# A transformer layer on one Trainium2 core: host order of x, norm weight spread by TensorE, and a written order of the engines for the first token tiles

## The chip, the core and the metric

The kernel runs on one core of a Trainium2 chip. The metric is the device time of one execution in microseconds (us); lower is better. The core has TensorE (in the profile PE for matmuls, PEld for the load of their stationary operand), VectorE (DVE), ScalarE (ACT), GpSimd (POOL) and SyncE (SP), which here only issues transfers. Each takes its instructions in order; semaphores join them. A difference of about 0.2% is what measurements of this kernel can tell from none.

## What is computed

One layer of an encoder on 1024 tokens of width 1024, in float32. Cut to what matters here:

```
h = x + 0.5 * swiglu(rms_norm(h, ffn1_norm), w_gate, w_up, w_down)   # d_ff 2816
u = rms_norm(h, mix_norm); two attention branches, gated; h = h + merged @ w_out
h = h + 0.5 * swiglu(rms_norm(h, ffn2_norm), ...)
y = rms_norm(h, final_norm)

swiglu: (silu(x @ w_gate) * (x @ w_up)) @ w_down
rms_norm: x * rsqrt(mean(x*x) + 1e-6) * g
```

The change touches the first norm, the start of the first `x @ w_gate` and `x @ w_up`, and the addresses of x and of the output.

## The kernel before

**Tokens.** The 1024 tokens form a grid of 16 rows and 64 columns. A token tile t (128 tokens) is the block of 8 columns over all rows; its rows of x lie in 16 runs of 8 tokens (L41). The output is written by the same pattern (L42, L1179). `res(t)` (L153) is the home of tile t in SBUF: four tiles `fx`, four quarters of `fa`.

**Precision.** Every operand of a product is kept as two parts: `split` (L88) has ScalarE cast the high part (L89) and VectorE subtract it for the low part (L90). `mm3` (L138) multiplies high by high, high by low, and low by high: three matmuls of 128 x 128 by 128 x 512 (L141, L143, L145) for each 128 of the contraction.

**Products.** The projections go by a Strassen scheme with seven products P1 to P7 (`products`, L233). The right operands are made from the turned, normed tiles: B11 and B21 (tiles 0 to 3) are there first, the others need tiles 4 to 7. For each group i of hidden units and m (gate, up) one product is four times `mm3`. P1 and P2 of groups 0 to 2 come first in the sequence (L239), since they need only B11 and B21. `prep` (L270) loads weights and splits them; for groups 1 and 2 of these the weights come through `ahead` (L261); `run` (L332) preps a little ahead and multiplies.

**The opening.** L590 to L602: SyncE issues x0, the norm weight (read 128 times over, 512 KB, L109), x1 to x3, the first gate and up blocks (`raw`), x4 to x7, and the second gate and up blocks. `transition` (L160) then takes the tiles in turn. `normed` (L112): ScalarE sums squares (L119), GpSimd makes the scale (L122, L123), VectorE multiplies by scale and weight (L125). `to_strassen` (L189): TensorE turns the tile by eight transposes into two banks (`turned`, L129), ScalarE and VectorE split the two banks into B11 and B21, and for tiles 0 to 3 ScalarE also keeps unsplit copies in `res` (L204, L205). For tiles 4 to 7 VectorE forms T1, T2 and what later becomes T3 and T4 (L209 to L215) and each is split. `behind` (L341) lets ten steps of the products run after each tile from tile 3 on. A scheduler puts all this in an order for each engine; engines keep to that order on the chip. `strassen_rest` (L221) and the rest of the products follow.

**Banks.** There are four PSUM banks "d" and four "g"; the turns use "d", the first products "g".

Of the kernel before, what the change touches and what calls it, by code (L numbers as in the profile page):

```python
# [25 lines left out]
NEG = -1.0e30  # L26
BIG = 1.0e38
# [9 lines left out]
def trunk_kernel(ctx, tc, x, n1, wg1, wu1, wd1, nm, win, rpb, sink, wa, wb, wo,  # L37
# [3 lines left out]
    x2 = x.rearrange("o (r b w) d -> (o b) r w d", b=NTT, w=8)  # L41
    out2 = out.rearrange("o (r b w) d -> (o b) r w d", b=NTT, w=8)  # L42
# [69 lines left out]
    def normed(h, gb, xs=None, parts=1):  # L112

        xs = xs4() if xs is None else xs
        w = D // parts
        cols = [slice(i * w, (i + 1) * w) for i in range(parts)]
        st = const.tile([P, 4], F32, tag="st", bufs=4, name=nm_("st"))
        for i, c in enumerate(cols):
            nc.scalar.activation(xs[:, c], h[:, c], AF.Square, scale=D ** -0.5, accum_out=st[:, i:i + 1])  # L119
# [3 lines left out]
        nc.gpsimd.tensor_tensor(st[:, 2:3], st[:, 0:1], nhalf, op=ALU.pow)  # L123
        for c in cols:
            nc.vector.scalar_tensor_tensor(out=xs[:, c], in0=h[:, c], scalar=st[:, 2:3], in1=gb[:, c],  # L125
                                           op0=ALU.mult, op1=ALU.mult)
        return xs

# [31 lines left out]
    def transition(pre, gain, turn_tile, post, halves=1, spare=()):  # L160


        h, xs = {}, {}
        n = NTT // halves
        for base in range(0, NTT, n):
            for t in (base, base + 1):
                h[t] = pre(t)
            xs[base] = normed(h.pop(base), gain)
            yield
            for t in range(base, base + n):  # L170
                if t + 2 < base + n:
                    h[t + 2] = pre(t + 2)
                if t + 1 < base + n:
                    xs[t + 1] = normed(h.pop(t + 1), gain, spare_xs() if t + 1 in spare else None)
# [13 lines left out]

    def to_strassen(t, xs):  # L189
# [5 lines left out]
        def put(o, src, eng=None):  # L195
            h, l = rhs(o)
            split(h[:, :, cols], l[:, :, cols], src, eng)
# [35 lines left out]
    def products(src, n, after, at_end, extra, ring):  # L233
# [36 lines left out]
        def prep(q):  # L270
# [11 lines left out]
            r1, r2 = raws[i, m, 0], raws[i, m, 1]  # L282
            a11, a12, a21, a22 = r1[:, :512], r1[:, 512:], r2[:, :512], r2[:, 512:]
# [13 lines left out]
        def multiply(q):  # L297
            i, p, m = seq[q]
            w = lhs.pop(q)
            h, l = rhs(RIGHT[p])  # L300
            first = p in ("P1", "P2", "P5")
            if p in ("P1", "P6", "P7", "P4"):
                if i == 2 and p == "P6":
                    first = True
                if first:
                    bks[i]["W", m] = bank("d" if i == 2 and p == "P1" else "g")
                b = bks[i]["W", m]
            elif p == "P2":
                if i == 2:
                    bks[i]["X", m] = bks[i]["W", m]  # L310
                    first = False
                else:
# [19 lines left out]
        def run():  # L332
            for q in range(len(seq)):
                prep_until(q + (1 if q < 4 else 2 if q < len(early) else 8))
                yield from multiply(q)
# [3 lines left out]
        return load, prep_until, run(), load_ahead  # L339

    def behind(prods):  # L341

        run, load_ahead = prods[2:]
# [222 lines left out]
    def down_ffn(wd, src):  # L566
# [4 lines left out]
        for t in range(NTT):  # L571
            loads.setdefault(2 + t, []).append(lambda d, t=t: nc.sync.dma_start(res(t), src(t)))
# [11 lines left out]
    down = down_ffn(wd1[0], lambda t: x2[t])  # L584
    hg = hidden(wg1[0], wu1[0], down.at_end)

    def load_x(t):
        nc.sync.dma_start(res(t), x2[t])

    load_x(0)  # L590
    gain = load_gain(n1[0])
    for t in range(1, 4):
        load_x(t)
    for m in range(2):
        hg[0](0, m, 0)
    for t in range(4, NTT):
        load_x(t)
    for m in range(2):
        hg[0](0, m, 1)
    drain(transition(res, gain, to_strassen, behind(hg), spare=(2, 3)))  # L600
# [560 lines left out]
    down = down_ffn(wd2[0], lambda t: h_d[t * P:(t + 1) * P, :])  # L1161
# [13 lines left out]
    def finish(t):  # L1175
        y = normed(res(t), gain, raw4() if t in (5, 7) else None, 2)
        for n in range(2):
            sl = slice(n * 512, (n + 1) * 512)
            nc.sync.dma_start(out2[t][:, :, sl], y[:, sl])  # L1179
# [9 lines left out]
def _consts():  # L1189
# [22 lines left out]
    tok = np.arange(T).reshape(ROWS, NTT, 8)  # L1212
    rope = rope[:, :, tok.transpose(1, 0, 2).reshape(-1)]
# [29 lines left out]
```

## Time and profile before

| | us |
|---|---|
| median of 3 runs | 1969.58 (1968.11 to 1970.52) |
| the profiled execution | 1971.38 |
| its span (first to last instruction) | 1969.4 |
| TensorE busy in the span | 1929.7 |
| VectorE, ScalarE busy | 1435.6, 952.4 |
| first transpose; first product | 9.35; 24.36 |
| last store of the output issued | 1964.78 |

In a row of a timeline the first number is the start in us from the span's start, the second the duration, then engine, line, operation, tile written and tiles read, shape, and in brackets how long the engine had been idle and what ended it. A row with x4 stands for four that follow each other. A group's row (from the page) gives busy time, mean ns, and idle time ahead of it with the releaser. A row of a window gives its stretch, its length, the busy time (and count) of TensorE, its weight load, VectorE, ScalarE and GpSimd, then granted clock, DMA share and GB/s. A row with three durations separated by slashes gives minimum, median and maximum in ns and the first and last start.

### The profile page before, as it was taken

The page shows a single profiled execution, that of the slowest core. Times are in us where ns is not written, and L with a number is a line of the kernel's source. Part 1 is how long each engine was busy: PE and PEld are TensorE (multiplying, and loading weights), DVE is VectorE, ACT ScalarE, POOL GpSimd, SP SyncE. Part 2 cuts the span into 40 slices and gives each one's busy share as a digit, 9 for nine tenths or more (in the row PEclk, how much of TensorE's full clock was granted, in tenths as well). Part 3 has the DMA queues.
Part 4 walks back from the last instruction along what each step waited for, and adds up shares of the span by engine and source line. Part 5 has one row for each costly group of instructions (what it writes and reads, how often), then busy time and mean ns, then how long its engine had stood idle before and what let it go on. Part 6 is the DMA issues. An engine that isn't in the chain of part 4 may idle for free. (4 is left out here: it accounts for less than half of the span.)

```text
span 1969.4 us, 25670 instructions
## 1 busy us (share of the span) xinstructions
PE 1929.7 (98%) x8968; PEld 1608.5 (82%) x8968; DVE 1435.6 (73%) x2503; ACT 952.4 (48%) x1846; POOL 338.1 (17%) x469
## 2 busy tenths in 40 slices
PE   6999999999999999899999999999999999999997
PEld 5888888888888888788888888878888888888886
DVE  6976566558967688578888866989766556569864
ACT  7433333334446543467787873356333333344452
POOL 1010001003400112111022134510101001005110
PEclk9999999999999999999999999999999999999999
DMA  8433323368333568553368675545523332493341
GB/s 210 141 116 102 118 86 107 123 221 271 92 118 124 168 190 268 173 171 94 84 161 176 177 240 192 182 139 156 149 87 107 107 102 95 139 356 105 117 141 53
DMA packets 234784, 293.45 MB, mean 149 GB/s; under 512 B 14208, under 2 KB 161024, under 8 KB 234656
## 3 DMA queue, kind: packets, MB, share of 16 engines
q1 hardware_dynamic: 206816, 206.24, 34.9%
q0 software_dynamic: 27840, 85.58, 13.2%
q8 instruction: 71, 1.16, 0.2%
q14 instruction: 57, 0.47, 0.1%
HBM read 205.16 MB, written 86.70 MB: 148 GB/s over the span
## 5 line engine op out<-in xcount | busy, mean ns | idle before, releaser
L141 PE MATMUL g<-ar,ws 128*128 128x512 f32 x1184 | 444.8, 397 | 3.6 <-ACT xs L870 1.9
L143 PE MATMUL g<-ar,ws 128*128 128x512 f32 x1184 | 438.2, 391 | 0.1
L145 PE MATMUL g<-ar,ws 128*128 128x512 f32 x1184 | 436.5, 391 | 0.3 <-DVE ws L90 0.3
L90 DVE TENSOR_TENSOR ws<-raw,ws 128x512 fp32r<-128x512 f32 (+1 forms) x329 | 237.3, 727 | 177.0 <-ACT ws L89 175.7
L89 ACT CAST ws<-raw 128x512 fp32r<-128x512 f32 (+1 forms) x331 | 209.5, 638 | 295.3 <-PE d L145 122.0
L141 PE MATMUL d<-ar,ws 128*128 128x512 f32 x680 | 262.4, 390 | 0.5 <-ACT ws L89 0.5
L145 PEld LDWEIGHTS g<-ar,ws 128*128 128x128 f32 x1184 | 223.2, 189 | 48.2 <-DVE ws L90 0.7
L145 PE MATMUL d<-ar,ws 128*128 128x512 f32 x680 | 261.9, 389 | 0.6 <-DVE ws L90 0.5
L143 PEld LDWEIGHTS g<-ar,ws 128*128 128x128 f32 x1184 | 223.4, 189 | 47.5 <-DVE ar L90 0.5
L143 PE MATMUL d<-ar,ws 128*128 128x512 f32 x680 | 262.0, 389 | 0.0
L141 PEld LDWEIGHTS g<-ar,ws 128*128 128x128 f32 x1184 | 218.2, 189 | 43.3 <-ACT xs L870 2.7
L145 PEld LDWEIGHTS d<-ar,ws 128*128 128x128 f32 x680 | 127.6, 188 | 27.5 <-DVE ws L90 1.1
L141 PEld LDWEIGHTS d<-ar,ws 128*128 128x128 f32 x680 | 127.6, 188 | 27.5 <-ACT ws L89 1.1
L143 PEld LDWEIGHTS d<-ar,ws 128*128 128x128 f32 x680 | 127.6, 188 | 26.4
L356 POOL DMA_DIRECT2D hid<-fx x96 | 52.1, 542 | 503.6 <-DVE fx L398 379.6
L90 DVE TENSOR_TENSOR ws<-ar,ws 128x512 fp32r<-128x512 f32 x114 | 108.1, 955 | 4.5 <-ACT ws L89 4.5
L89 ACT CAST ar<-raw 128x512 fp32r<-128x512 f32 (+1 forms) x83 | 56.0, 678 | 91.2 <-PE g L143 53.1
L90 DVE TENSOR_TENSOR ws<-fa,ws 128x512 fp32r<-128x512 f32 x76 | 52.6, 692 | 53.3 <-ACT ws L89 52.9
L141 PE MATMUL g<-ws,ws 128*128 128x512 f32 x232 | 91.0, 392 | 0.0
L145 PE MATMUL g<-ws,ws 128*128 128x512 f32 x232 | 90.4, 390 | 0.0
L143 PE MATMUL g<-ws,ws 128*128 128x512 f32 x232 | 90.3, 389 | 0.0
L1016 ACT ACTIVATE fa<-fa,nmx 128x385 f32<-128x385 f32 (+3 forms) x128 | 75.5, 591 | 27.5 <-DVE nmx L1013 26.8
(232 smaller groups left out, 3515.1 us busy)
## 6 DMA issues: line engine op xcount, KB each, us to landing
raw<-hid SPq DMA_DIRECT2D x70, 512.0 KB
hid<-fx POOLq DMA_DIRECT2D x96, 256.0 KB, 2.6
raw<-in_ffn_w_up_dram SPq DMA_DIRECT2D x32, 512.0 KB
ar<-in_ffn_w_down_dram SPq DMA_DIRECT2D x32, 512.0 KB
raw<-in_ffn_w_gate_dram SPq DMA_DIRECT2D x28, 512.0 KB
hid<-fa POOLq DMA_DIRECT2D x54, 256.0 KB, 2.6
raw<-in_w_in_dram SPq DMA_DIRECT2D x27, 512.0 KB
ar<-zs_d POOLq DMA_DIRECT2D x48, 256.0 KB, 5.1
```

The costliest lines, as they stand in the source:

```text
L89: nc.scalar.copy(dst_hi, src)
L90: (eng or nc.vector).tensor_tensor(dst_lo, src, f32v(dst_hi), op=ALU.subtract)
L141: nc.tensor.matmul(b, lhs[0], r[0], start=first, stop=False, **kw)
L143: nc.tensor.matmul(b, lhs[0], r[1], start=False, stop=False, **kw)
L145: nc.tensor.matmul(b, lhs[1], r[0], start=False, stop=last, **kw)
L356: nc.gpsimd.dma_start(hid[PRODUCTS.index(p), i], src)
L1016: nc.scalar.activation(pr, pr, AF.Exp, scale=-1.0, bias=nmx[:, s:s + 1], accum_out=ssum[:, s:s + 1])
```

## The change

1. The host brings x into tile order, so that a tile of x is 128 rows that follow each other, and the host undoes that order on the output. Loads of x (also those for the residual) and stores of the output become plain row ranges.
2. The norm weight of the first norm is loaded as 8 x 128 (4 KB) as the first transfer. TensorE turns it into columns; eight transposes of a column that is read 128 times give the weight for all partitions, and VectorE copies it out of PSUM in two halves. Twelve transposes of the identity stand before and twelve after.
3. x0, x1, the first gate block, x2, x3, the first up block, then x4 to x7 is the order of the first transfers. P1 and P2 of group 0 need no second half of the weights any more; it is loaded after tile 4.
4. The first four products (P1, P2 of group 0, gate and up) are done in two halves of 256 columns: `half(q)` multiplies tiles 0 and 1 only; `run` later does the columns of tiles 2 and 3.
5. For tiles 0 to 3 the order of VectorE, ScalarE and TensorE is written by hand and kept (`first_tiles`); from tile 4 on the scheduler decides.

```diff
+ORDER = np.arange(T).reshape(ROWS, T // P, 8).transpose(1, 0, 2).reshape(-1)
-    x2 = x.rearrange("o (r b w) d -> (o b) r w d", b=NTT, w=8)
-    out2 = out.rearrange("o (r b w) d -> (o b) r w d", b=NTT, w=8)
+    x2 = x.rearrange("b t d -> (b t) d")
+    out2 = out.rearrange("b t d -> (b t) d")
...
-            for half in range(2):
+            for half in range(1 if i == 0 and p in ("P1", "P2") else 2):
                 if (i, m, half) not in raws:
                     load(i, m, half)
...
+            ts = slice(0, 512) if n is None else slice(n * 256, n * 256 + 256)
             for c in range(4):
                 cs = slice(c * P, (c + 1) * P)
-                mm3([b], c == 0 and first, c == 3, (w[:, cs], w[:, 512:][:, cs]),
-                    [(h[:, c, :], l[:, c, :])], skip_group_check=True)
+                mm3([b[:, ts]], c == 0 and first and n != 1, c == 3, (w[:, cs], w[:, 512:][:, cs]),
+                    [(h[:, c, ts], l[:, c, ts])], skip_group_check=True)
...
+            if t == 4:
+                for m in range(2):
+                    prods[0](0, m, 1)
...
+    def first_gain(g):
+        rows = main.tile([NC8, P], F32, tag="s1", bufs=1, name=nm_("rows"))
+        nc.sync.dma_start(rows, g.rearrange("(c f) -> c f", c=NC8))
+        b = bank("g")
+        for _ in range(12):
+            nc.tensor.transpose(b[:, :P], ident, ident)
+        b = bank("d")
+        nc.tensor.transpose(b[:, :NC8], rows, ident[:NC8, :NC8])
+        cols = const.tile([P, NC8], F32, name="cols")
+        nc.vector.tensor_copy(cols, b[:, :NC8])
+        gb = const.tile([P, 1152], F32, tag="gain", bufs=1, name=nm_("gain"))
+        for half in range(2):
+            b = bank("g")
+            for c in range(4):
+                k = 4 * half + c
+                nc.tensor.transpose(b[:, c * P:(c + 1) * P], cols[:, k:k + 1].to_broadcast([P, P]), ident)
+            nc.vector.tensor_copy(gb[:, half * 512:half * 512 + 512], b)
+        b = bank("g")
+        for _ in range(12):
+            nc.tensor.transpose(b[:, :P], ident, ident)
+        return gb[:, :D]
...
+    def first_tiles():
+        st, pts = {}, {}
+        def put(t, o):
+            put_cols((B11, B21)[o], slice(t * P, (t + 1) * P), pts[t][o])
+        def keep(t):
+            for o in range(2):
+                nc.scalar.copy(res(t)[:, o * 512:(o + 1) * 512].rearrange("p (c t) -> p c t", c=4), pts[t][o])
+        def turn(t):
+            pts[t] = turned(scaled(*st[t], res(t), gain))
+        def half(q):
+            hg[1](q + 1)
+            drain(hg[4](q, 0))
+        for t in range(3):
+            st[t] = root(res(t), None if t < 2 else spare_xs())
+        turn(0)
+        put(0, 0)
+        st[3] = root(res(3), spare_xs())
+        turn(1)
+        put(1, 0)
+        for q in range(2):
+            half(q)
+        for t in range(2):
+            put(t, 1)
+            keep(t)
+        turn(2)
+        half(2)
+        put(2, 0)
+        put(2, 1)
+        half(3)
+        turn(3)
+        put(3, 0)
+        put(3, 1)
+        for t in (2, 3):
+            keep(t)
+
+    with tc.manual_schedule(engines={DVE, Activation, PE}):
+        first_tiles()
+    tc.no_sync_barrier()
+    post = behind(hg)
+    xs = {4: normed(res(4), gain)}
+    for t in range(4, NTT):
+        if t + 1 < NTT:
+            xs[t + 1] = normed(res(t + 1), gain)
+        to_strassen(t, xs.pop(t))
+        post(t - 1)
+    post(NTT - 1)
```

Here `root` is the first half of `normed` (ScalarE's sum of squares and GpSimd's scale), `scaled` the second (VectorE's multiplication), and `put_cols` one split of a turned bank into B11 or B21.

More of the change, by code (lines that the diff above doesn't have):

```diff
@@ L123, in normed, with scaled @@
         nc.gpsimd.tensor_tensor(st[:, 2:3], st[:, 0:1], nhalf, op=ALU.pow)
-        for c in cols:
+        return xs, st
+    def scaled(xs, st, h, gb, parts=1):
+        w = D // parts
+        for i in range(parts):
+            c = slice(i * w, (i + 1) * w)
             nc.vector.scalar_tensor_tensor(out=xs[:, c], in0=h[:, c], scalar=st[:, 2:3], in1=gb[:, c],
@@ L304, in multiply @@
                     first = True
-                if first:
+                if first and n != 1:
                     bks[i]["W", m] = bank("d" if i == 2 and p == "P1" else "g")
@@ L583, in trunk_kernel @@
         new_ar(g)
-    down = down_ffn(wd1[0], lambda t: x2[t])
+    down = down_ffn(wd1[0], x2)
     hg = hidden(wg1[0], wu1[0], down.at_end)
     def load_x(t):
[L588 to L592, printed above, removed]
+        nc.sync.dma_start(res(t), x2[t * P:(t + 1) * P, :])
+    def first_gain(g):
[19 more added lines that the diff above has]
+        return gb[:, :D]
@@ L593, in trunk_kernel @@
+    gain = first_gain(n1[0])
+    for t in range(2):
         load_x(t)
-    for m in range(2):
-        hg[0](0, m, 0)
+    hg[0](0, 0, 0)
+    for t in range(2, 4):
+        load_x(t)
+    hg[0](0, 1, 0)
     for t in range(4, NTT):
         load_x(t)
-    for m in range(2):
-        hg[0](0, m, 1)
-    drain(transition(res, gain, to_strassen, behind(hg), spare=(2, 3)))
+    def first_tiles():
[19 more added lines that the diff above has]
+            half(q)
+        for t in range(2):
+            put(t, 1)
[10 more added lines that the diff above has]
+            keep(t)
```

54 lines of the change are left out of this document (32 added, 22 removed).

## The prediction

> **What bounds the kernel now.** I read the page first (how full TensorE is), then TensorE's waits, then the first 51 us engine by engine, because the change touches only these and the last transfers.
>
> ```profile
> span 1969.4 us, 25670 instructions
> PE 1929.7 (98%) x8968; PEld 1608.5 (82%) x8968; DVE 1435.6 (73%) x2503; ACT 952.4 (48%) x1846; POOL 338.1 (17%) x469
> ...
> L145 PE MATMUL d<-ar,ws 128*128 128x512 f32 x680 | 261.9, 389 | 0.6 <-DVE ws L90 0.5
> ```
>
> TensorE is busy for 98% of the span, so the kernel ends earlier or later by what TensorE waits. The L145 row names one wait on VectorE for a weight's low part (DVE ws L90). Its place follows from the timelines of TensorE, VectorE (DVE) and ScalarE (ACT).
>
> ```profile
> 9.35 1.97 PE L134 MATMUL d<-ident,xs 128*128 128x128 f32 x8 [9.35 <-DVE xs L125]
> 18.91 3.83 PE L134 MATMUL d<-ident,xs 128*128 128x128 f32 x16 [3.68 <-ACT fx L204]
> 24.36 0.79 PE L141 MATMUL g<-ar,ws 128*128 128x512 f32 x1 [1.63 <-ACT ar L89]
> 26.88 0.78 PE L143 MATMUL g<-ar,ws 128*128 128x512 f32 x1
> 28.87 0.39 PE L141 MATMUL g<-ar,ws 128*128 128x512 f32 x1
> 29.10 0.40 PE L143 MATMUL g<-ar,ws 128*128 128x512 f32 x1
> 34.34 1.03 PE L134 MATMUL d<-ident,xs 128*128 128x128 f32 x8
> 48.99 1.03 PE L134 MATMUL d<-ident,xs 128*128 128x128 f32 x8
> 50.12 0.50 PE L145 MATMUL d<-ar,ws 128*128 128x512 f32 x1
> ```
>
> ```profile
> 8.01 1.28 DVE L125 SCALAR_TENSOR_TENSOR xs<-fx,st,gain 128x1024 f32<-128x1024 f32 x1 [8.01 <-POOL st L123]
> 17.55 2.48 DVE L90 TENSOR_TENSOR ar<-d,ar 128x512 fp32r<-128x512 f32 x4
> 42.80 1.28 DVE L125 SCALAR_TENSOR_TENSOR xs<-fa,st,gain 128x1024 f32<-128x1024 f32 x1
> 44.00 0.69 DVE L209 TENSOR_TENSOR fa<-d,fx 128x512 f32<-128x512 f32 x1
> 49.38 0.69 DVE L90 TENSOR_TENSOR ws<-ahead,ws 128x512 fp32r<-128x512 f32 x1
> 58.39 0.68 DVE L287 TENSOR_TENSOR s<-raw 128x512 f32<-128x512 f32 x1
> ```
>
> The first product starts at 24.36, the stream holds from 26.88, and matmuls then follow each other every 0.23 us (28.87 to 29.10). At 50.12 it stops once more: the matmul there needs the low part that VectorE makes from 49.38 to 50.07. This is the eighth weight, product P2 of group 1, m = 1. From there to 790 us the waits of TensorE are one row:
>
> ```profile
> PE d L141 <- ACT ws L89: 0.5, 1, 0.5
> ```
>
> So the opening is worth what **VectorE** needs to reach that one subtraction; the start of the first product decides nothing by itself. VectorE's account: in the built order 48 instructions stand from the first norm (8.01) to that subtraction, 8 norms with 1.2 us from one to the next (42.80 to 44.00) and 40 of 512 columns at 0.60 (four in 2.48, the last 0.08 being pipeline): 8 x 1.2 + 40 x 0.6 = 33.6 us. From 8.01 to 50.07 are 42.06, so VectorE idles 8.4 there.
>
> **The change part by part.** The built order of the changed program has the same 48 instructions between the first norm and the low part of the eighth weight (only their order differs; the three new copies of the norm weight stand ahead). After the 147th TensorE instruction of before, at 50.1, TensorE's order is the same to the end. So the sum is: where VectorE starts, 33.6 us of work, and its idle time in the new order.
>
> *Loads.* These rows give ScalarE's waits for x, and the pace of the transfers:
>
> ```profile
> 5.87 1.06 ACT L119 ACTIVATE xs<-fx 128x1024 f32<-128x1024 f32 x1 [3.86 <-DMA fx<-in_x_dram]
> 9.77 1.06 ACT L119 ACTIVATE xs<-fx 128x1024 f32<-128x1024 f32 x1 [2.75 <-DMA fx<-in_x_dram]
> 12.02 1.06 ACT L119 ACTIVATE xs<-fx 128x1024 f32<-128x1024 f32 x1 [1.10 <-DMA fx<-in_x_dram]
> 15.26 1.05 ACT L89 CAST ar<-d 128x512 fp32r<-128x512 f32 x2
> ```
>
> ```profile
> 18.00:24.00 6.00, 3.83 (x16) 3.14 (x16) 4.66 (x9) 5.73 (x12) 0.79 (x2) 1.00 1.04 236
> 26.00:35.00 9.00, 9.00 (x42) 7.63 (x41) 7.65 (x12) 8.02 (x15) 2.35 (x4) 1.00 1.17 287
> 1121.50:1124.50 3.00, 3.00 (x20) 2.69 (x19) 2.77 (x10) 2.39 (x8) 0.57 (x1) 1.00 0.79 298
> 1299.60:1302.00 2.40, 2.40 (x12) 1.97 (x12) 2.40 (x5) 2.40 (x7) 0.80 (x2) 1.00 1.00 403
> ```
>
> ```profile
> 1121.05 0.80 SPq L1103 DMA_DIRECT2D fx<-h_d  x2
> ...
> 1298.80 2.89 SPq L1167 DMA_DIRECT2D h_d<-fx  x4
> ```
>
> A scattered tile of x (512 KB) takes 2.2 us (236 GB/s), a half block of weights 1.8 (287). For a contiguous tile the bounds are 2.2 and 1.3 (the contiguous h_d stores at 403); I take 1.75, from the window that reads h_d back (298). The 512 KB norm weight leaves the head of the queue for a 4 KB one, and the first gate block moves ahead of x2. Landings, from 5.87 for x0 with a little off for its shorter issue: x0 5.6, x1 7.4, gate 9.2, x2 10.95, x3 12.7, up 14.5. The second gate and up halves move behind x and the first blocks ahead; their first reader is P5 (L287 at 58.39), and the e_d copies behind them are read near 960 us, so this costs nothing.
>
> *Norm weight by TensorE.* Nine transposes, a tiny copy and two 512-column copies follow a 4 KB load that lands near 3.7. At 0.22 a transpose (1.97 for eight) and 0.68 a copy they end near 7.7, when the first norm is ready anyway (5.6 + 2.14, the step from 5.87 to 8.01). Nothing on the path: the first tile waits later for another reason, with over 3 us of cover.
>
> *Fixed order.* Here is the cost. Every engine takes its queue in order, and I follow VectorE:
> - norm 0 from 7.8 to 9.0. The next VectorE instruction is the low part of tile 0. It needs ScalarE's high part, which now stands behind the square sum of x2: that starts when x2 lands, 10.95, ends at 12.05, the high part takes 0.6. **Idle 3.65**, to 12.65.
> - norm 1 stands behind it: 13.25 to 14.5. TensorE turns tile 1 (first half after 1.1), ScalarE casts to 16.3: **idle 1.85**. The first product starts at 16.8, 7.6 us before 24.36.
> - Four low parts to 18.7. The fifth needs a cast that stands behind two keep copies, one of which waits for VectorE's own 18.1 to 18.8: **idle 1.2**, to 19.9.
> - norm 2 from 20.5 to 21.8. TensorE turns tile 2 after the 24 half matmuls that stand ahead (16.8 to about 22); turn and cast end at 23.5: **idle 1.15**.
> - norm 3 to 26.6, turn, cast: **idle 1.4**, to 27.9; two low parts to 29.1.
> - norm 4 needs tile 4's square sum, which ScalarE has behind two casts and all four keep copies of tiles 2 and 3 (27.3 to 30.1; two casts take 1.05 at 15.26, so 0.48 from one to the next), though x4 landed near 16. Square sum and GpSimd's steps take 2.14: **idle 3.2**, to 32.3.
> - Then VectorE runs full, but for **1.0** near 44, where ScalarE loads the table for Silu ahead of a cast that VectorE needs (row below), and 0.15 of rests.
>
> ```profile
> L395 ACT ACT_TABLE_LOAD  x2: 1283/1283/1283, 38.1 to 1340.4; - x2
> ```
>
> Idle together 13.6, against 8.4. VectorE reaches the end of that low part at 7.8 + 33.6 + 13.6 = 55.0 instead of 50.07: **+4.9**. TensorE, early with its halves, waits meanwhile: turn 4 (norm 4 ends at 33.6) stands in its queue ahead of 21 half matmuls that are ready, and turn 6 waits for a norm that VectorE does after 2 norms and 8 subtractions (40.8).
>
> *Halves.* 96 matmuls of 256 columns for 48 of 512. Four of 256 columns in the row below give 0.12 each (the row at 1010.87 follows 0.49 later):
>
> ```profile
> 1010.38 0.65 PE L1048 MATMUL g<-ws,fx 128*128 128x256 f32 x4
> 1010.87 0.34 PE L1008 MATMUL d<-ar 128*128 128x384 f32 x1
> ```
>
> 96 x 0.12 - 48 x 0.23 = 0.5 us more work, hidden in TensorE's waits; without these it costs 0.5.
>
> *Warming transposes.* In before 16 transposes run at 0.22 to 0.24 each at 18.91 and the first products come late after each other, too; at 34.34 a transpose takes 0.13. [...] At 0.21 a half matmul turn 2 comes at 22.1 to 22.4, at 0.12 it comes at 21.85, when norm 2 ends: a term of 0.3 to 0.8, not 5.
>
> *Output.* The last two stores decide the end:
>
> ```profile
> 1964.78 1.20 SPq L1179 DMA_DIRECT2D out_dram<-raw  x2
> ```
>
> ```profile
> L663 SPq DMA_DIRECT2D h_d<-fa x4: 319/338/339, 654.0 to 673.3; - x4
> ```
>
> 0.6 us an issue, with a row pattern of three dimensions; contiguous rows take 0.32 to 0.34 in the h_d stores (L663). The last issue can end 0.2 to 0.3 earlier and its packets follow more closely; bounds 0 and 0.9, I take **-0.5**. The second load of x, for the residual, is contiguous now and hidden: between 51 and 790 us TensorE waits for no transfer (the one row above).
>
> Sum +4.9 - 0.5 = +4.4. The profiled execution took 1971.38 (span 1969.4 and 1.98 around it), 1.8 above the median of the runs; the difference is put on the median: 1969.58 + 4.4 = **1974.0**.
>
> **Rivals.**
> *The early start pays* (faster). TensorE alone would need from 16.8 to the place it has at 50.12 the 147 instructions of before less 16 turns done: 83 matmuls x 0.23, 48 transposes x 0.13, some 2.5 for those at the lower clock and 0.5 for the halves = 28.4, so 45.2: -4.9, with the stores -5.4: 1964.2. It decides when VectorE idles under 3.8 us (45.2 - 7.8 - 33.6). For it: the first product does come 7.6 us earlier, and the page calls TensorE the full engine. Against it: the two stalls before norm 4 and behind x2 alone are 6.9. Chance 0.06.
> *Smaller loss*: x at the pace of the stores (three tiles x 0.45: x2 1.35 earlier) and halves at 0.12 (0.3): idle 12.0, so +3.3, +2.8 with the stores: 1972.4. Chance 0.22.
> *Larger loss*: contiguous rows bring nothing (2.2 a tile: x2 1.35 later) and the lower clock lasts past turn 3 (8 transposes and a half product, 0.9): idle 15.8, so +7.1, +6.6 with the stores: 1976.2. Chance 0.14.
> *It does not what it says*: the new order of x moves the same bytes, and the output's order is undone outside; a scheduler that puts the queues otherwise is excluded by the built order. No chance of its own.
>
> **How the numbers follow.** The forecast has 0.58, by itself 1972.9 to 1975.3. The bound of 0.2%, which is what a measurement tells from no change, is 3.9 us: 1973.5. Of the forecast's chance I put 0.44 above it; with the larger loss slower has 0.58, within has 0.36 (0.14 and the smaller loss), faster 0.06. The range is 1971.8 to 1976.8: it leaves out the early start, and the outer part of the two losses.
>
> **What would show it.** Right: the first half matmul near 17; VectorE idle 3 us or more before the norm of tile 4, released by GpSimd behind ScalarE; TensorE waiting before turns 4 and 6, until about 33.6 and 40.8; the last wait of the opening at about 55 on a DVE ws row. Wrong: the low part of the eighth weight before 51 us, or no TensorE wait after 30 us (the early start), or a first norm of tile 1 well before 13 us. If TensorE gains in the opening and the end is still later, a wait beyond 60 us has grown, which the unchanged order there speaks against.

## The result, and the profile after

The changed kernel takes 1975.29 us (median of 7 runs, 1973.82 to 1979.87), the kernel before 1969.58 beside it: a ratio of 1.0033, 95% interval 1.0021 to 1.0045. It is slower, by 5.7 us between the medians. The profiled execution took 1975.28 with a span of 1973.1, against 1971.38 and 1969.4: +3.9.

The page of the changed kernel, as of before:

```profile
span 1973.1 us, 25840 instructions
PE 1936.7 (98%) x9049; PEld 1614.8 (82%) x9049; DVE 1437.2 (73%) x2506; ACT 952.3 (48%) x1846; POOL 340.3 (17%) x469
```

TensorE still fills 98% of the span. Its waits between 62 and 790 us are again next to nothing (waits of TensorE in that stretch):

```profile
PE g L152 <- DVE fa L752: 0.2, 1, 0.2
```

So the opening is where to look, and there VectorE. These are the rows of its timeline that begin with an idle stretch, and the last one is the low part of the eighth weight (49.38 in before):

```profile
7.32 1.28 DVE L132 SCALAR_TENSOR_TENSOR xs<-fx,st,gain 128x1024 f32<-128x1024 f32 x1 [0.21 <-POOL st L125]
11.30 0.69 DVE L92 TENSOR_TENSOR ar<-d,ar 128x512 fp32r<-128x512 f32 x1 [2.69 <-ACT ar L91]
...
15.00 0.69 DVE L92 TENSOR_TENSOR ar<-d,ar 128x512 fp32r<-128x512 f32 x1 [1.82 <-ACT ar L91]
...
18.64 0.69 DVE L92 TENSOR_TENSOR ar<-d,ar 128x512 fp32r<-128x512 f32 x1 [1.14 <-ACT ar L91]
...
21.96 1.29 DVE L92 TENSOR_TENSOR ar<-d,ar 128x512 fp32r<-128x512 f32 x2 [0.76 <-ACT ar L91]
...
26.47 1.29 DVE L92 TENSOR_TENSOR ar<-d,ar 128x512 fp32r<-128x512 f32 x2 [1.43 <-ACT ar L91]
30.92 1.28 DVE L132 SCALAR_TENSOR_TENSOR xs<-fa,st,gain 128x1024 f32<-128x1024 f32 x1 [3.16 <-POOL st L125]
32.97 1.28 DVE L132 SCALAR_TENSOR_TENSOR xs<-fa,st,gain 128x1024 f32<-128x1024 f32 x1 [0.77 <-POOL st L125]
...
44.29 0.69 DVE L92 TENSOR_TENSOR ar<-fa,ar 128x512 fp32r<-128x512 f32 x1 [1.04 <-ACT ar L91]
...
51.22 0.69 DVE L92 TENSOR_TENSOR ar<-fa,ar 128x512 fp32r<-128x512 f32 x1 [0.23 <-ACT ar L91]
...
54.23 0.68 DVE L92 TENSOR_TENSOR ws<-ahead,ws 128x512 fp32r<-128x512 f32 x1
```

It starts 54.23 - 49.38 = 4.85 later than before. The idle stretches behind norm 0 add up to 13.0, and nearly all end on ScalarE or on a scale that waits for ScalarE. ScalarE's timeline has two of the causes:

```profile
9.64 1.06 ACT L121 ACTIVATE xs<-fx 128x1024 f32<-128x1024 f32 x1 [2.15 <-DMA fx<-in_x_dram]
...
10.70 0.57 ACT L91 CAST ar<-d 128x512 fp32r<-128x512 f32 x1
...
26.81 2.07 ACT L654 COPY fx<-d 128x512 f32<-128x512 f32 x4
28.72 1.11 ACT L121 ACTIVATE xs<-fa 128x1024 f32<-128x1024 f32 x1
```

The high part of tile 0 (10.70) stands behind the square sum of x2, which waits for its transfer until 9.64 (1.3 of the 2.69; the rest, 1.37 in e2 below, is the turn and the cast). The square sum of tile 4 (28.72) stands behind the four keep copies.

TensorE's timeline shows the clock by the pace of equal instructions:

```profile
6.22 1.47 PE L632 MATMUL g<-ident 128*128 128x128 f32 x12
8.66 1.09 PE L145 MATMUL d<-ident,xs 128*128 128x128 f32 x8 [0.97 <-DVE xs L132]
13.23 1.97 PE L145 MATMUL d<-ident,xs 128*128 128x128 f32 x8 [3.48 <-DVE xs L132]
15.54 0.58 PE L152 MATMUL g<-ar,ws 128*128 128x256 f32 x1 [0.34 <-ACT ws L91]
...
18.87 0.41 PE L154 MATMUL g<-ar,ws 128*128 128x256 f32 x1
19.08 0.41 PE L156 MATMUL g<-ar,ws 128*128 128x256 f32 x1
...
22.05 0.28 PE L154 MATMUL g<-ar,ws 128*128 128x256 f32 x1
22.17 0.28 PE L156 MATMUL g<-ar,ws 128*128 128x256 f32 x1
...
32.35 1.06 PE L145 MATMUL d<-ident,xs 128*128 128x128 f32 x8 [1.75 <-DVE xs L132]
...
40.40 1.94 PE L145 MATMUL d<-ident,xs 128*128 128x128 f32 x8 [2.79 <-DVE xs L132]
...
54.97 0.50 PE L156 MATMUL d<-ar,ws 128*128 128x512 f32 x1 [0.48 <-DVE ws L92]
```

Twelve transposes at 6.22 take 1.47 (0.12 each) and turn 0 takes 1.09: full pace. TensorE then idles 3.48, and turn 1 takes 1.97 again; half matmuls follow each other every 0.21 until about 19.6 and every 0.12 from then on. The last three rows are TensorE's waits for VectorE ahead of turn 4, of turn 6 and of the product with the eighth weight. Windows of the same kernel, whose third number from the end is the granted clock:

```profile
12.90:19.60 6.70, 6.01 (x25) 5.32 (x26) 3.73 (x7) 4.40 (x9) 0.93 (x2) 0.50 1.08 356
...
39.00:40.00 1.00, 0.00 (x0) 0.00 (x0) 1.00 (x2) 1.00 (x3) 0.92 (x2) 1.00 0.00 0
40.20:43.40 3.20, 3.00 (x11) 2.76 (x12) 3.05 (x6) 3.17 (x6) 0.48 (x1) 0.50 0.00 0
```

The clock was granted, lost by the end of an idle stretch of 3.48 us, held at 0.50 for some 6.8 us, and lost once more, by the end of the wait of 2.79 for turn 6, for 3.4 us. In before TensorE's pace is slow up to 28 us; the stream then holds, and from there to 100 us the column of the granted clock reads 1.00. Ahead of that the column does not tell the pace: it reads 1.00 from 18 to 24 us in before too, where 16 transposes take 0.24 each. There the pace has to be read.

The end of the kernel, VectorE and SyncE (before: 1964.00 and 1964.78):

```profile
1967.54 1.41 DVE L132 SCALAR_TENSOR_TENSOR raw<-fa,st,gain 128x512 f32<-128x512 f32 x2 [2.02 <-POOL st L125]
1968.32 0.99 SPq L1275 DMA_DIRECT2D out_dram<-raw  x2
```

**Where the 3.9 come from.** +4.85 in the opening. Of these 1.3 are given back on the way, since the last norm is only 3.54 later. Counted back from its last instruction, TensorE is 4.83 later all the way from 60 to 600 us, 3.98 at 700, 4.61 at 1000, 2.91 at 1173 and 3.55 from 1350 on. So it goes down and up, and only behind 600 us. The largest step lies in this window, in before and after:

```profile
1100.00:1200.00 100.00, 96.63 (x496) 82.40 (x495) 67.99 (x160) 71.12 (x142) 29.38 (x18) 0.98 0.61 196
```

```profile
1100.00:1200.00 100.00, 97.25 (x510) 82.44 (x509) 68.47 (x171) 72.87 (x149) 28.54 (x18) 1.00 0.59 197
```

Before lost some clock there (0.98), after did not; nothing of the change stands there. These are single executions, and the drift behind 600 us is not put down to the change. From the end of the last norm to the end of the span are 4.15 (1973.1 - 1968.95) against 3.98, and around the span 2.18 against 1.98. 4.85 - 1.3 + 0.2 + 0.2 = 3.9.

### The profile page after: what moved, and what is told of

It reads as the page before. It is cut to its first block, busy times and chain, and to the rows that moved or that the text cites. A ratio compares the mean times of both kernels' runs of the same rounds, so it can differ in the third digit from the quotient of the medians.

```text
span 1973.1 us, 25840 instructions
## 1 busy us (share of the span) xinstructions
PE 1936.7 (98%) x9049; PEld 1614.8 (82%) x9049; DVE 1437.2 (73%) x2506; ACT 952.3 (48%) x1846; POOL 340.3 (17%) x469
## 5 line engine op out<-in xcount | busy, mean ns | idle before, releaser
L152 PE MATMUL g<-ar,ws 128*128 128x512 f32 (+1 forms) x1200 | 448.0, 394 | 1.6 <-ACT ar L1026 0.3
L154 PE MATMUL g<-ar,ws 128*128 128x512 f32 (+1 forms) x1200 | 441.2, 389 | 0.9 <-POOL ar L92 0.5
L156 PE MATMUL g<-ar,ws 128*128 128x512 f32 (+1 forms) x1200 | 440.1, 389 | 0.7 <-DVE ws L92 0.7
L156 PEld LDWEIGHTS g<-ar,ws 128*128 128x128 f32 x1200 | 226.5, 189 | 48.8 <-DVE ws L92 1.9
L154 PEld LDWEIGHTS g<-ar,ws 128*128 128x128 f32 x1200 | 226.7, 189 | 47.8 <-DVE ar L92 1.0
L152 PEld LDWEIGHTS g<-ar,ws 128*128 128x128 f32 x1200 | 221.5, 189 | 41.9 <-ACT ws L91 1.1
```

The costliest lines, as they stand in the source:

```text
L152: nc.tensor.matmul(b, lhs[0], r[0], start=first, stop=False, **kw)
L154: nc.tensor.matmul(b, lhs[0], r[1], start=False, stop=False, **kw)
L156: nc.tensor.matmul(b, lhs[1], r[0], start=False, stop=last, **kw)
```

## The experiments

The theory is the one on record: VectorE's idle time in the written order makes the loss. The rivals are TensorE's own work with the halves and the clock, and the parts of the change that stand outside the written order. Besides the time, each kernel gives the start of the eighth weight's low part, which is read against 49.38 (before) and 54.23 (after). It comes from one profiled execution of each. In kernels that load x2 alike and wait for it, its square sum starts between 9.17 and 9.75, so half a microsecond in this column can be the transfer alone. Every kernel but e5 then keeps its distance to the others within 0.1 us up to 600 us and drifts by one or two behind: from the low part to the end of the last norm take 1912.9 to 1917.5 (e4b 1919.8).

| kernel | low part, start | median us | ratio to before |
|---|---|---|---|
| changed kernel | 54.23 | 1975.29 | 1.0033 (1.0021 to 1.0045) |
| e1_sq45 | 53.62 | 1974.10 | 1.0024 (1.0016 to 1.0033) |
| e2_hi0 | 54.29 | 1974.99 | 1.0026 (1.0017 to 1.0036) |
| e3_all | 51.56 | 1972.69 | 1.0016 (1.0006 to 1.0025) |
| e4b_full | 60.30 | 1985.57 | 1.0085 (1.0071 to 1.0099) |
| e5_nowarm | 54.60 | 1974.29 | 1.0023 (1.0013 to 1.0033) |
| e6_xorder | 47.16 | 1967.12 | 0.9982 (0.9973 to 0.9991) |
| e7_gain | 48.08 | 1969.57 | 1.0002 (0.9993 to 1.0011) |
| e9_busy | 56.58 | 1976.70 | 1.0036 (1.0023 to 1.0048) |
| e10_fill | 53.51 | 1974.72 | 1.0026 (1.0017 to 1.0035) |
| e11_allfill | 48.04 | 1967.89 | 0.9994 (0.9985 to 1.0002) |
| e12_ahead | 46.49 | 1965.41 | 0.9975 (0.9966 to 0.9984) |

### Does VectorE's queue decide? (e9_busy)

```diff
         to_strassen(t, xs.pop(t))
+        if t == 5:
+            dump = main.tile([P, 512], F32, tag="s1", bufs=1, name=nm_("dump"))
+            for _ in range(8):
+                nc.vector.tensor_copy(dump, xs[t + 1][:, :512])
```

> The changed kernel with eight more copies of 512 columns on VectorE, into a buffer that nothing reads, behind the norm of tile 6, where VectorE has no idle time but 1.04 near 44. Theory (VectorE's queue decides the opening): 8 x 0.60 = 4.8, less the idle time of 1.04 that they can stand in: eighth weight's low part at 58.3 to 59.7, time 3.3 to 4.8 above 1975.3: 1978.6 to 1980.1. Rival (TensorE or ScalarE is as late by itself, VectorE has slack): low part less than 2 later, time below 1977.3.

The group of the copies, and the low part in VectorE's timeline:

```profile
L698 DVE COPY dump<-xs x8: 411/419/447, 40.3 to 50.4; 128x512 f32<-128x512 f32 x8
```

```profile
56.58 0.68 DVE L92 TENSOR_TENSOR ws<-ahead,ws 128x512 fp32r<-128x512 f32 x1
```

A copy is shorter than the 0.60 that was put in (0.42, and the next instruction starts 0.34 after it, 47.90 to 48.24). So 8 x 0.34 = 2.7 were added, and the low part came 2.35 later. Up to the norm of tile 6 this execution was 0.46 ahead of the changed kernel (38.52 against 38.98, x2 having landed earlier), so that 2.8 were added from there on: all of it arrives. The median rose by 1.4 only, within the rival's bound, but by its interval it can't be told from 2.35; in the profiled executions the changed kernel spends 1.05 more than e9 behind the last norm, where the two do not differ (4.15 against 3.10, see "Output" below). VectorE's queue sets the eighth weight; the expectation failed on the price of a copy.

### ScalarE's order alone (e1_sq45, e2_hi0, e3_all)

```diff
+        for t in (4, 5):                 # e1, e3
+            st[t] = root(res(t))
         turn(3)
```

```diff
-        for t in range(3):               # e2, e3
-            st[t] = root(res(t), None if t < 2 else spare_xs())
+        for t in range(2):
+            st[t] = root(res(t))
         turn(0)
         put(0, 0)
+        st[2] = root(res(2), spare_xs())
```

```diff
         for t in range(2):               # e3
             put(t, 1)
+        for t in range(2):
             keep(t)
```

> The changed kernel, but ScalarE does the square sums of tiles 4 and 5 ahead of the casts of tile 3, where it waits for turn 3 (from about 22 to 26 us), instead of behind the four keep copies of tiles 2 and 3. Theory (VectorE's idle time in the written order makes the loss): the idle 3.16 and 0.77 ahead of norms 4 and 5 go; the low part of the eighth weight ends 2.5 to 3.9 earlier than 54.91, so at 51.0 to 52.4, and the time is 2.5 to 3.9 below the changed kernel's 1975.3: 1971.4 to 1972.8. Rival (TensorE's own work in the opening, with the halves, decides): the low part moves by less than 1 us, the time stays within 1974.3 to 1976.

> The changed kernel, but on ScalarE the square sum of x2 stands behind the high part of tile 0 instead of ahead of it. Theory: VectorE's idle 2.69 ahead of the low part of tile 0 (at 11.30) becomes the turn and the cast alone, 1.3 to 1.5, and everything behind it moves by 1.2 to 1.4: eighth weight's low part at 53.5 to 53.8, time near 1974.0, just about what a measurement tells. Rival (the 3.16 ahead of norm 4 takes it up, since the square sum of tile 4 is late for another reason): low part at 54.9, time 1975.3.

> The changed kernel with three edits on ScalarE's order: square sums of tiles 4 and 5 ahead of the casts of tile 3; square sum of x2 behind the high part of tile 0; the high parts of the second halves of tiles 0 and 1 both ahead of the four keep copies of these tiles. Theory: VectorE's idle time to the eighth weight's low part falls from 13.9 to 7.5 to 8.5, the low part ends at 48.3 to 49.6, 5.3 to 6.6 earlier: 1968.7 to 1970.0, about the kernel before. Rival (the gains do not add: TensorE with its halves and turns becomes what is late): low part at 51 or later, time at 1971.5 or more.

All three fell short. In e1 the 3.16 ahead of norm 4 did vanish, and the low part still came only 0.6 earlier, as the rival had it. In e2 the first idle stretch shrank as said (VectorE's timeline), and the low part did not move at all:

```profile
9.75 0.69 DVE L92 TENSOR_TENSOR ar<-d,ar 128x512 fp32r<-128x512 f32 x1 [1.37 <-ACT ar L91]
```

The windows say what took the gain, first e1, then e2:

```profile
44.00:48.00 4.00, 4.00 (x11) 3.14 (x10) 4.00 (x6) 0.00 (x0) 0.77 (x1) 0.50 0.32 83
```

```profile
45.80:49.00 3.20, 3.20 (x9) 2.43 (x8) 3.20 (x6) 0.00 (x0) 0.77 (x1) 0.53 0.32 102
```

TensorE, idle a little before (3.94 us in e1; 1.45, 0.97 and 0.47 in e2), runs at half clock just where its products are wanted. In e3 the chain can be followed, ScalarE first, then VectorE:

```profile
46.89 0.58 ACT L396 COPY fa<-g 128x512 f32<-128x512 f32 x1 [5.08 <-PE g L156]
```

```profile
48.55 0.69 DVE L92 TENSOR_TENSOR ar<-fa,ar 128x512 fp32r<-128x512 f32 x1 [2.06 <-ACT ar L91]
```

ScalarE waits 5.08 for a product, the casts behind that copy are late, and VectorE idles 2.06. That the clock makes this wait is so far argued from the windows; the next two kernels test it.

### Keeping TensorE's clock (e10_fill, e11_allfill)

Both fill idle stretches of TensorE with work that changes no result: transposes of the identity into a bank that a turn then overwrites, and in e11 also matmuls with a zero operand that add nothing to a running sum.

```diff
             pt = bank("d")
+            for _ in range(fill if half == 0 else 0):     # 24 for turn 1, 18 for turn 6 (e10); 16 for turn 1 (e11)
+                nc.tensor.transpose(pt[:, :P], ident, ident)
```

```diff
             nc.tensor.matmul(b, lhs[0], r[1], start=False, stop=False, **kw)
+        for _ in range(fill):                             # e11, in group 1, P2, m = 0: 18
+            nc.tensor.matmul(banks[0][:, :P], ident, zero.to_broadcast([P, P]), start=False, stop=False, **kw)
```

> The changed kernel with 24 more transposes of the identity ahead of turn 1 and 18 ahead of turn 6, into banks that these turns overwrite: they fill TensorE's two long idle stretches and compute nothing. Theory (idle TensorE loses the granted clock, 0.50 in the trace from 12.9 to 19.3 and 40.15 to 43.45; VectorE's idle time in the written order still holds most of the loss): granted clock 1.00 from 0 to 60, eighth weight's low part 0.7 to 1.7 ahead of 54.91, time 1973.5 to 1974.6. Rival (the clock is what the +4.9 is made of): low part at 50 to 52, time 1970.5 to 1972.5. Second rival (a by-effect without weight): low part within 0.3 of 54.91, time 1975.3.

> The kernel with the three edits of ScalarE's order (e3), and TensorE's idle stretches filled: 16 transposes of the identity ahead of turn 1, and 18 matmuls with a zero operand that add nothing ahead of the wait near 37. Theory (in e3 the gain of the new order was lost again to the granted clock: 0.50 from 39.0 to 45.6, ScalarE's copy waits 5.08 for TensorE there and VectorE 2.06 for ScalarE): clock 1.00 in both places, VectorE's 2.06 goes, eighth weight's low part ends at 47.7 to 49.7 instead of 52.24, time 2.5 to 4.5 below the 1972.7 of e3: 1968.2 to 1970.2, level with the kernel before or ahead of it. Rival (VectorE would wait there at full clock too): low part at 51.5 to 52.5, time 1972 to 1973.

e10, on the changed kernel, keeps the clock, and gains 0.7 in the opening (54.23 to 53.51), which is the theory's lower end; its median of 1974.72 stands just outside the range named:

```profile
40.00:44.00 4.00, 3.89 (x21) 2.95 (x18) 2.96 (x6) 3.97 (x8) 0.00 (x0) 1.00 0.46 135
```

Of the 0.7, 0.45 are turn 1 at the full pace (VectorE idles 1.37 ahead of tile 1's low part, not 1.82) and 0.28 the transfer of x2 (square sum at 9.36, not 9.64). The filling ahead of turn 6 brought nothing: the idle stretches behind it stay 1.04 and 0.24. So in the changed kernel as it is, the clock is about 0.5 of the +4.85, and the order is the rest. e11, on e3, is another matter. A window of e3 and the same of e11:

```profile
40.00:44.00 4.00, 2.85 (x7) 2.29 (x8) 4.00 (x7) 1.81 (x4) 0.77 (x1) 0.50 0.05 6
```

```profile
40.00:44.00 4.00, 3.90 (x17) 3.04 (x17) 4.00 (x7) 0.81 (x3) 0.77 (x1) 1.00 0.17 66
```

TensorE's timeline of e11 has the second filling (the trace has two records for each of the 18 matmuls, the first two of them at 34.88), ScalarE's the copy, VectorE's the low part:

```profile
35.56 3.95 PE L158 MATMUL d<-zero,ident 128*128 128x128 f32 x34
```

```profile
43.37 0.59 ACT L404 COPY fa<-g 128x512 f32<-128x512 f32 x1 [3.19 <-PE g L160]
```

```profile
48.04 0.68 DVE L92 TENSOR_TENSOR ws<-ahead,ws 128x512 fp32r<-128x512 f32 x1
```

The copy starts at 43.37 instead of 46.89, and the low part comes 3.5 earlier than in e3; the time falls from 1972.69 to 1967.89. Each filling has about half of the 3.5: VectorE's 2.06 became 0.16 behind the second, and the idle stretches behind turns 1 and 2 went from 2.16 and 1.52 to 1.36 and 0.38 behind the first. The spread falls too: e3's twelve runs lie between 1969.0 and 1978.4, the longest at the lowest granted clock (0.991, mean of the run), e11's eleven between 1966.4 and 1969.2 at 0.996 to 0.998. The fillings are the only difference between the two kernels, so the clock is shown to be what had held e3 back. For e1 and e2, which were not filled, it is argued from their windows.

### Parts of the change (e6_xorder, e7_gain, e5_nowarm, e4b_full)

e6 is the kernel before with the items on x and the output alone (item 1 of the change). e7 adds `first_gain` with its 24 transposes and the order of the loads, and keeps `transition`, so the scheduler sets the order:

```diff
-    load_x(0)
-    gain = load_gain(n1[0])
+    gain = first_gain(n1[0])
+    for t in range(2):
+        load_x(t)
+    hg[0](0, 0, 0)
```

> The kernel before with x and the output in tile order alone; norm weight, loads' order and the scheduler's order stay. Theory (contiguous tiles land in 1.4 to 1.75 instead of 2.2 us each, VectorE's idle time ahead of norms 1 and 2 shrinks): eighth weight's low part ends 1.5 to 2.5 ahead of the 50.07 of before; the stores bring -0.5 by the prediction, or nothing by the changed kernel's trace, where the end lies 4.15 behind VectorE's last norm instead of 3.98: time 1966.8 to 1968.3. Rival (the cast of the first weight, whose load stands behind, holds VectorE anyway): low part within 0.5 of 50.07, time 1969 to 1970.

> The kernel before with x and the output in tile order, the norm weight spread by TensorE (with the 24 transposes) and the loads in the changed order, but without the written order and the halves: the scheduler sets the engines' order as before. Theory (the written order is what costs; loads and norm weight by themselves gain): eighth weight's low part ends 1.5 to 3.5 ahead of the 50.07 of before, at 46.5 to 48.6, time 1966.5 to 1968.5. Rival (a TensorE that was warmed early and then idles gets the granted clock 0.5, as in the changed kernel from 12.9 to 19.3, and this takes the gain): low part within 1 us of 50.07, time 1969 to 1971.

e6 came out as the theory had it, and is faster than before. ScalarE's timeline has the pace of x, VectorE's the low part:

```profile
9.13 1.06 ACT L121 ACTIVATE xs<-fx 128x1024 f32<-128x1024 f32 x1 [0.16 <-DMA fx<-in_x_dram]
...
10.47 1.06 ACT L121 ACTIVATE xs<-fx 128x1024 f32<-128x1024 f32 x1 [0.20 <-DMA fx<-in_x_dram]
```

```profile
47.16 0.69 DVE L92 TENSOR_TENSOR ws<-ahead,ws 128x512 fp32r<-128x512 f32 x1
```

1.34 from one tile to the next (2.2 in before), 2.2 off the opening, 3.1 off the median. e7 missed: the opening gained 1.3 and the time nothing. VectorE's first row behind the copies of the norm weight shows one reason:

```profile
12.15 0.69 DVE L92 TENSOR_TENSOR ws<-raw,ws 128x512 fp32r<-128x512 f32 x1 [5.46 <-ACT ws L91]
```

The scheduler put a weight's low part ahead of norm 0, whose scale GpSimd had at 6.9 (the step that starts at 6.37 takes 0.57). ScalarE casts that weight only at 11.52, right behind the square sums of x2 and x3, which wait for their transfers. The rival of a lost clock is not out: TensorE idles 6.98 ahead of its first turns and does 16 transposes at half clock (0.50 from 14 to 18 us). What took the other 1.3 us in the median was not settled.

e5 takes the two loops of twelve transposes out of `first_gain`:

> The changed kernel without the 24 transposes of the identity. Theory (VectorE's order decides, the clock at turn 0 is a term of tenths): turn 0 takes the long time again (1.97 instead of 1.09), which stands beside the wait for the square sum of x2; eighth weight's low part within 0.5 of 54.91, time 1974.8 to 1975.8. Rival (the transposes earn what they are there for): low part past 56, time 1976.5 or more. Second rival (warmed early, TensorE only loses the granted clock again, 0.50 from 12.9 to 19.3): low part near 53.5, time near 1974.

Turn 0 takes 1.97 again, as expected. The low part moved by 0.4, within the theory's 0.5; the median moved by -1.0, inside both spreads but 0.5 below the theory's range and near the second rival's 1974, whose low part of 53.5 did not come. That the warming transposes are worth nothing here either way is as far as this goes.

e4b takes the halves away. (A first form, e4_full, at 1986.21, also copied the first finished products into the home of tiles 4 to 7 ahead of their norms, so that these norms read other data; e4b keeps those copies where they were.) With them it takes away steps of the products that run behind tiles 3 and 4: 5 and 7 instead of 10. `prods is hg` holds for the second swiglu too, so that TensorE's order changes there as well.

```diff
-                drain(run, 10)
+                drain(run, {3: 5, 4: 7}.get(t, 10) if prods is hg else 10)
...
         put(3, 1)
+        for q in range(2):
+            drain(hg[4](q))              # 512 columns, instead of half(q) on 256
```

> The changed kernel without the halves: the first products run on 512 columns, behind the split of tile 3; the orders of VectorE and ScalarE are kept but for one copy of a finished product behind, not ahead of, the norm of tile 4's successor. The first product then starts near 27 instead of 15.5. Theory as put in the prediction (the start of the first product decides nothing by itself, the halves are 0.5 of hidden work): eighth weight's low part within 1 us of 54.91, time 1974.3 to 1976.3. Rival (TensorE's early start did earn something, because the copies of its finished products stand in VectorE's queue): low part at 57 to 58, time 1977.3 to 1978.5.

> The changed kernel without the halves: the first four products run on 512 columns, the first two of them right behind the split of tile 3; the written order of VectorE and ScalarE is kept. The first product then starts near 27 instead of 15.5. Theory as put in the prediction (the start of the first product decides nothing by itself, the halves are 0.5 of hidden work): eighth weight's low part within 1 us of 54.91, time 1974.3 to 1976.3. Rival (TensorE's early start did earn something, because copies of its finished products and casts stand in the queues of VectorE and ScalarE): low part at 56 to 58, time 1976.5 to 1978.5.

The largest miss: the low part came 6.1 later than in the changed kernel, and the median 10. VectorE's timeline and a window:

```profile
38.25 0.69 DVE L222 TENSOR_TENSOR fa<-d,fx 128x512 f32<-128x512 f32 x1 [2.93 <-PE d L145]
...
60.30 0.68 DVE L92 TENSOR_TENSOR ws<-ahead,ws 128x512 fp32r<-128x512 f32 x1
```

```profile
24.00:28.00 4.00, 2.58 (x10) 1.95 (x10) 1.96 (x3) 1.19 (x3) 0.00 (x0) 0.50 0.00 0
```

Without the halves TensorE has nothing but two turns to do from turn 1 to the split of tile 3, stands at half clock, and is then late: turn 4 stands in its queue behind the first products, and VectorE idles 2.93 for it. That is half of the 6.1; the rest are longer waits for ScalarE's casts (1.89 instead of 1.43 behind turn 3, 1.56 instead of 0.23 near 58). Even the rival's price (56 to 58) was too low. The 10 of the median is not the price of the halves: e4b's TensorE lies 6.05 behind the changed kernel's from 60 to 600 us, 7.4 at 1320 and 11.2 from 1380 on, and these 3.8 fall where the second swiglu has its first products, with fewer steps behind the tiles. What the fewer steps do in the opening was not run apart from the halves.

### A version that beats both (e12_ahead)

e11 with VectorE's norms one tile ahead, so that the idle time behind a turn and a cast has work in it (the splits of tiles 2 and 3 and the square sums of tiles 4 and 5 are set between them accordingly, and 12 transposes ahead of the first half product replace the 16 ahead of turn 1):

```diff
+        norm(0)
         turn(0)
+        norm(1)
         put(0, 0)
...
+        norm(2)
         for t in range(2):
             put(t, 1)
         for t in range(2):
             keep(t)
+        norm(3)
         turn(2)
+        turn(3)
         half(2)
```

> The kernel of e11 (ScalarE's order mended, TensorE's idle stretches filled) with the norms one tile ahead in VectorE's queue: norm 1 ahead of the low part of tile 0, norm 2 ahead of the second halves of tiles 0 and 1, norm 3 ahead of the low parts of tile 2; turn 3 ahead of the third half product; 12 transposes of the identity ahead of the first half product, 18 matmuls with a zero operand as in e11. Theory (what VectorE idles in e11, 1.37, 1.36 and 1.43 behind each turn and cast, is work that can stand there): idle time falls by 2 to 3, eighth weight's low part at 45.9 to 47.4 instead of 48.72, time 1.3 to 2.8 below 1967.9: 1965.1 to 1966.6, ahead of the kernel before. Rival (TensorE is the bound by then): low part within 0.7 of 48.72, time 1967.2 to 1968.2.

VectorE's timeline:

```profile
9.32 1.29 DVE L132 SCALAR_TENSOR_TENSOR xs<-fx,st,gain 128x1024 f32<-128x1024 f32 x1 [0.47 <-POOL st L125]
...
46.49 0.69 DVE L92 TENSOR_TENSOR ws<-ahead,ws 128x512 fp32r<-128x512 f32 x1
```

Norm 1 stands where the idle time was, the low part comes 2.9 ahead of before, and the time is 1965.41: 0.9975 of before (0.9966 to 0.9984), as expected. Against e6, which changes nothing but the order of x and of the output, that is 1.7 less in the median, with intervals that overlap (0.9973 to 0.9991), and the two profiled executions took the same (1965.12 and 1965.11). That the written order earns more than x in tile order alone is not shown.

## Why the prediction was right, and where not

The forecast was 1974.0, within 1971.8 to 1976.8, and slower as the likeliest; measured are 1975.29. The mechanism and nearly every term stand in the trace.

- **VectorE's queue decides.** Right for the changed order, by e9. Forecast: start 7.8, 33.6 of work, idle 13.6, end 55.0. Measured: start 7.32, end 54.91. The signs that were named came too: first half matmul at 15.54, TensorE waiting ahead of turns 4 and 6 until 32.35 and 40.40, and at 54.97 for the eighth weight.
- **The idle terms**, forecast and measured: behind the square sum of x2 3.65 and 2.69; turn 1 and cast 1.85 and 1.82; behind the keep copies 1.2 and 1.14; turn 2 1.15 and 0.76; turn 3 1.4 and 1.43; norm 4 3.2 and 3.16; near 44 1.0 and 1.04; rests 0.15 and 0.23. Not foreseen: 0.77 ahead of norm 5. Some 0.9 more are the ends of VectorE's last instruction ahead of each idle stretch (0.69 long where the next starts after 0.60): the 8.4 of before, a difference, holds them, the 13.6, a list, left them out. An end within 0.1 of the forecast is in part luck: the start was 0.5 earlier and the terms of the list 1.3 smaller, and these two took it back.
- **Loads.** x2 was forecast for 10.95 and its square sum started at 9.64. The pace of contiguous tiles is 1.34 (e6), the lower bound of 1.3 to 2.2, not the 1.75 taken. It made the first stretch 1.0 shorter.
- **"The start of the first product decides nothing by itself"**, and halves that cost 0.5 if uncovered: this step fell. Without the halves, and with fewer steps of the products behind tiles 3 and 4, the low part comes 6.1 later (e4b). In the sum it did no harm, since the change has the halves; it would have misjudged a change that leaves them out.
- **Warming transposes.** The forecast took the first turns at the longer time of before, and named 0.21 and 0.12 a half matmul, worth 0.3 to 0.8 between them. Both paces came: 0.21 up to about 19.6, where the granted clock reads 0.50 (the "lower clock" of the rivals), and 0.12 behind. But turn 0 took 1.09: the rows at 6.22 and 8.66 show the full pace behind nothing but transposes, and without the 24 turn 0 takes 1.97 (e5). The result was near the forecast because TensorE lost the clock in the next idle stretch: 0.50 for 6.8 us with 3.48 of idle time, and for 3.4 us with 2.79. The clock is worth 0.45 in the opening by e10, where 0.3 to 0.8 had been put. The size is luck: it lies at turn 1, and at turn 2, where the forecast had it, VectorE idles 0.76 in both kernels.
- **Output.** Forecast -0.5 within 0 and -0.9; the profiled execution has +0.2. The issue is shorter as forecast (two in 0.99, not 1.20). But from the end of the last norm to the end of the span the kernels with contiguous stores take either 3.05 to 3.10 (e1, e3, e4b, e6, e7, e9, e11, e12) or 4.15 to 4.19 (the changed kernel, e2, e5, e10), against 3.98 in before. In the second group one part of the last stores lands 1.1 us behind the rest (1972.12 against 1971.01 in the changed kernel); in the first the last landings lie within 0.04. So the term is -0.9, or +0.2 with a late landing. What makes it late was not found, and with one profile of each kernel it can't be told whether it belongs to the kernel or to the execution.
- **The rest of the kernel** was taken as unchanged, and up to 600 us it is; behind that the profiled execution gave back 1.3, most likely in large part by the clock that before lost between 1100 and 1200 us (0.98 there, 1.00 in the changed kernel).
- **Rivals.** The early start does not pay: VectorE idled 13.0, not under 3.8. The smaller loss had x2 at its landing but not the half matmuls at 0.12 before 19.6. In the sum of the early start, 147 instructions should be 150 by the trace (three products more, 0.7 us), which changes no choice.

Between the medians the loss is 5.7, in the profiled executions 3.9, in the opening 4.85. The profiled execution of before lies 1.8 above its median, that of the changed kernel at its own: that is the step from 3.9 to 5.7. The opening's agrees with the interval of the ratio (4.1 to 8.9 us); what the median has above it stays open. e6, e7 and the changed kernel together say which part costs. In the opening x in tile order brings 2.2, norm weight and loads take 0.9 of that back in the scheduler's order, and the written order with the halves costs 6.15 (48.08 to 54.23). In the medians it is 3.1, nearly all of it, and the rest.

## What to carry to other kernels

When an order is written by hand, follow the engine that decides instruction by instruction, and ask of each instruction ahead of its inputs whether it waits for something unrelated: a square sum behind a transfer, a square sum behind four copies. When such a wait is removed and the time does not follow, look at the clock in the windows before giving the theory up: in e3 it stood at 0.50 from 40 to 44 us, and with TensorE's idle stretches filled (e11, 1.00 there) the low part came at 48.04 instead of 51.56. Compare two kernels at a place shortly behind the change, and not by the end alone: here the distance held from 60 to 600 us, and what came behind was of the size of the effects. Try the parts of a change alone: the plainest of them, x in tile order, gained 3.1 us.

## What the runs showed of the hardware

- In the changed kernel the first 12 transposes of the fp32 identity take 2.82 (from 1.35), the second 12 take 1.47 (from 6.22), and the eight of turn 0 behind them 1.09 (from 8.66). Without the 24, in e5, the eight of turn 0 take 1.97.
- In the changed kernel the granted clock is 0.50 from 12.9 to 19.6 and from 40.2 to 43.4; TensorE idles 3.48 up to 13.23 and 2.79 up to 40.40. In e2, which differs from it in one place of ScalarE's order, it is 0.50 from 12.0 to 18.5 and from 32.5 to 35.5, and 0.53 from 45.8 to 49.0. With the idle stretches filled (e10) it is 1.00 from 40 to 44.
- Contiguous 512 KB tiles of x follow each other every 1.34 us (e6, square sums from 9.13 and 10.47), scattered ones every 2.2 (before).
- In the opening of the changed kernel three first steps of a scale on GpSimd (L124) begin beside a norm of VectorE, at 7.58, 12.40 and 31.05; they take 1.11, 0.86 and 1.23 and end 0.08 to 0.09 behind that norm. GpSimd's timeline of the changed kernel:

```profile
6.29 0.22 POOL L124 TENSOR_SCALAR st<-st 128x1 f32<-128x1 f32 x1 [4.99 <-ACT xs L121]
...
31.05 1.23 POOL L124 TENSOR_SCALAR st<-st 128x1 f32<-128x1 f32 x1 [0.17 <-ACT xs L121]
```

The same step takes 0.22 alone and 1.23 beside the norm that runs from 30.92 to 32.20. That is the 0.77 ahead of norm 5.
